# The last block of the down projection: block sizes, order of products, gate, residual and norm weight

## The chip, the cores and the metric

The kernel runs on one NeuronCore of a Trainium2 chip. The metric is device time in microseconds, the median of several executions. The profile is taken from one execution of its own. TensorE multiplies matrices into PSUM, VectorE and ScalarE work element by element on SBUF and PSUM, GpSimd on SBUF; DMAs are issued from SyncE's queue, and accumulating ones from GpSimd's.

## The reference

One layer of a streaming encoder over 512 tokens of width 2048, in float32, and a final RMSNorm. The change touches only its end:

```python
h = modulate(rmsnorm(x, g_norm_ffn[l]), sh2, sc2)
f = (jax.nn.silu(h @ w_ffn_gate[l]) * (h @ w_ffn_up[l])) @ w_ffn_down[l]
x = x + gt2[:, None, :] * f
return rmsnorm(x, g_norm_final)
```

The inner width is 5632. The x of the third line is called x1 here, gt2 is the gate row, and the final norm's weight is g_norm_final.

## The kernel before, in words

**Numbers in two parts.** Every float32 operand is split into hi (rounded to the format that TensorE takes at full rate) and lo (the rest), and a product is three matmuls, hi*hi, hi*lo and lo*hi (`mm3x`, line 938). ScalarE makes hi, VectorE makes lo (`split_into`, line 390); a part of weights is 128x1024.

**Seven products.** Gate, up and down are computed by a 2x2 scheme with seven products for eight (`seven`, line 862). The tokens are two halves (token blocks 0 and 1, and 2 and 3, 128 tokens each), the inner index is taken in groups of 512 (two halves of 256), and two column blocks of 512 make a pass. The left operands are seven tiles per 128 of the inner index. The products are called A11, n1, s2, n4, n3, A12 and A22, in this order; after each, a step named P1, G5, G6, G3, G7, P2 or G4 adds the two PSUM banks that are ready to the sums. The right operands come from four loads and a few sums on VectorE (`b11` to `t4`, lines 889 to 921).

**Down.** Its 11 groups are taken in blocks of `DOWN_BLOCKS` = 3, 3, 3, 2 (line 32). A block loads its left operands from DRAM (14 tiles of 256 KB per group), then makes two passes: columns 0 and 1 (qp = 0), columns 2 and 3 (qp = 1). The sums `fsum[t][q]` (16 tiles of 128x512) stay in SBUF. `later_block` (line 1085) adds each step's banks on VectorE; steps P1, P2 and G4 write column qa of the pass, the others qb. In the last block `finish` (line 1049), after the last addition to a tile, loads x1, multiplies by the gate and adds x1 (both VectorE), and squares with a sum per token (ScalarE). After all blocks the loop at line 1113 makes the norm's factor of each token block (`rstd_from`, line 442, small instructions of VectorE and one square root of ScalarE), multiplies by g_norm_final on GpSimd and by the factor on ScalarE, and stores.

**What sets the order.** Nothing is issued as it is called. `Program` (line 35) records every operation, derives due times backwards from TensorE's order in the program (`deadlines`, line 155), and lays out all five instruction streams with costs of its own (`cost`, line 114, the constants at lines 52 to 62; `schedule`, line 205). An operation goes when its inputs are ready by these costs and its output has a buffer; among those ready at once, the one due first. On the chip each engine then takes its stream in that fixed order. `fits` (line 240) decides whether a tile may be taken ahead of an earlier one of its kind; for hi and lo (3 buffers each) it may not (`IN_ORDER`, line 63, used at line 251). There are 69 buffers of 128x512.

Every instruction of the profile has line 357, where the streams are issued.

## Time and profile before

| | |
|---|---|
| median of 3 runs | 1924.98 us (1924.12 to 1926.82) |
| the profiled execution's own time | 1928.34 us |
| its span, first to last instruction | 1926.5 us |
| TensorE busy | 1813.8 us (94%), mean granted clock 0.978 |
| VectorE busy | 1552.2 us (81%) |
| ScalarE, GpSimd busy | 935.5 us (49%), 216.1 us (11%) |

Down runs from about 1440 to 1897 us of the span. PE is TensorE's matmuls, PEld its weight loads, DVE VectorE, ACT ScalarE, POOL GpSimd, SP SyncE; tiles are named without their numbers, so `b` is any 128x512 tile (sums, gates, x1), `acc` a PSUM bank, `raw` and `araw` loaded weights. The chain of waits follows the end of the program back to what released each step; the timeline lists an engine's instructions by start; instructions overlap by a little, so that the distance of two starts is less than a duration.

### The profile page before, as it was taken

How to read it: one execution, taken by the hardware profiler on the slowest of the kernel's cores; microseconds unless marked ns; L12 is line 12 of the kernel's file. 1: busy time of each engine (PE TensorE's matmuls, PEld its weight loads, DVE VectorE, ACT ScalarE, POOL GpSimd, SP SyncE). 2: the span in 40 equal slices, each digit the busy share in tenths (PEclk: the TensorE clock that was granted, in tenths of full speed). 3: DMA queues.
4: the chain of work that ended last, by engine and by line, in shares of the span. 5: the costliest groups of instructions: out<-in, count | busy, mean ns of one | idle time of the engine just before them, and what ended most of it. 6: DMA issues, size and time to landing. Idle time of an engine off the chain costs nothing.

```text
span 1926.5 us, 22784 instructions
## 1 busy us (share of the span) xinstructions
PE 1813.8 (94%) x8019; PEld 1482.8 (77%) x8019; DVE 1552.2 (81%) x1979; ACT 935.5 (49%) x1213; POOL 216.1 (11%) x192
## 2 busy tenths in 40 slices
PE   3899999899998999999999999999999999999993
PEld 2687877687776788888888788887887888888883
DVE  5897999789869878787877867877667878888898
ACT  6434784432237455454554545545444444333345
POOL 0000045500000010011100111001110000000015
PEclk9999999999998999999999999999999999999997
DMA  9997455599972688678867878876799785675922
GB/s 288 310 336 225 151 187 169 169 316 310 340 233 59 161 211 228 181 225 219 223 179 217 218 184 214 227 189 179 180 302 335 225 283 183 217 263 185 343 88 88
DMA packets 283587, 425.78 MB, mean 221 GB/s; under 512 B 20632, under 2 KB 119632, under 8 KB 283472
## 3 DMA queue, kind: packets, MB, share of 16 engines
q1 hardware_dynamic: 259536, 378.17, 59.4%
q0 software_dynamic: 23936, 46.14, 14.2%
q8 instruction: 63, 1.03, 0.2%
q14 instruction: 52, 0.43, 0.1%
HBM read 374.44 MB, written 49.81 MB: 220 GB/s over the span
## 4 chain that ended last, share of the span: by engine, by line
PE 72%; DVE 14%; DMA 8%; issue 3%; ACT 2%; SPq 1%; POOL 1%; ACTq 0%; DVEq 0%; POOLq 0%
PE acc L357 69%; DVE b L357 10%; DMA araw<-in_w_ada 5%; DVE lo L357 3%; PE mm L357 3%; DMA raw<-in_w_ada 1%; ACT b L357 1%; SPq L357 1%; DMA raw<-in_w_ffn_up 1%; ACT hi L357 1%; DVE araw L357 1%; POOL b L357 1%; DMA f<-b 1%; DMA b<-in_x 0%; DVE s L357 0%
## 5 line engine op out<-in xcount | busy, mean ns | idle before, releaser
L357 PE MATMUL acc<-hi,b 128*128 128x512 f32 x4208 | 1281.9, 393 | 10.3 <-DVE b L357 5.6
L357 PEld LDWEIGHTS acc<-hi,b 128*128 128x128 f32 x4208 | 792.0, 189 | 175.8 <-DVE b L357 7.0
L357 PE MATMUL acc<-lo,b 128*128 128x512 f32 x2104 | 791.8, 393 | 2.0 <-DVE lo L357 1.9
L357 ACT ACTIVATE hi<-raw 128x1024 fp32r<-128x1024 f32 (+2 forms) x289 | 298.7, 1035 | 482.8 <-PE acc L357 382.5
L357 DVE TENSOR_TENSOR lo<-raw,hi 128x1024 fp32r<-128x1024 f32 (+2 forms) x289 | 346.6, 1201 | 148.1 <-ACT hi L357 147.0
L357 PEld LDWEIGHTS acc<-lo,b 128*128 128x128 f32 x2104 | 398.0, 189 | 86.5 <-DVE lo L357 5.0
L357 ACT ACTIVATE hi<-araw 128x1024 fp32r<-128x1024 f32 x264 | 280.1, 1062 | 300.1 <-PE acc L357 270.7
L357 DVE TENSOR_TENSOR lo<-araw,hi 128x1024 fp32r<-128x1024 f32 x198 | 242.3, 1225 | 56.8 <-ACT hi L357 56.1
L357 DVE SCALAR_TENSOR_TENSOR b<-araw,c_act,b 128x512 f32<-128x512 f32 (+1 forms) x315 | 236.4, 756 | 17.1 <-DMA araw<-in_w_ada 12.8
L357 DVE TENSOR_TENSOR b<-b,b 128x512 f32<-128x512 f32 (+4 forms) x318 | 193.1, 635 | 11.7 <-ACT b L357 11.4
L357 PE MATMUL acc<-b,hi 128*128 128x512 f32 x608 | 191.5, 400 | 4.3 <-ACT b L357 3.6
L357 ACT ACTIVATE b<-b 128x512 fp32r<-128x512 f32 (+2 forms) x223 | 128.6, 595 | 83.0 <-DVE b L357 69.2
L357 PEld LDWEIGHTS acc<-b,hi 128*128 128x128 f32 x608 | 115.9, 192 | 30.7 <-ACT b L357 5.7
L357 POOL DMA_DIRECT2D araw<-in_w_ffn_up x44 | 53.1, 1206 | 628.9 <-DVE lo L357 628.1
L357 PE MATMUL acc<-b,lo 128*128 128x512 f32 x304 | 116.2, 396 | 0.7 <-DVE lo L357 0.7
L357 DVE SCALAR_TENSOR_TENSOR lo<-araw,hi 128x1024 fp32r<-128x1024 f32 x66 | 80.6, 1222 | 40.9 <-ACT hi L357 40.7
L357 POOL TENSOR_TENSOR b<-b,b 128x512 f32<-128x512 f32 x32 | 58.0, 1831 | 457.3 <-DVE b L357 430.8
L357 ACT ACTIVATE b<-acc 128x512 f32<-128x512 f32 x142 | 82.3, 593 | 55.0 <-PE acc L357 39.5
L357 DVE TENSOR_TENSOR araw<-araw,raw 128x1024 f32<-128x1024 f32 x88 | 106.9, 1221 | 0.9
L357 POOL DMA_DIRECT2D raw<-in_w_ffn_up x44 | 53.0, 1204 | 315.0 <-DVE lo L357 312.7
L357 DVE SCALAR_TENSOR_TENSOR araw<-araw,raw 128x1024 f32<-128x1024 f32 x66 | 80.0, 1220 | 5.9 <-DMA raw<-in_w_ffn_down 3.2
L357 PE MATMUL mm<-b,hi 128*128 128x512 f32 x192 | 63.3, 410 | 12.4 <-ACT b L357 11.0
(72 smaller groups left out, 909.0 us busy)
## 6 DMA issues: line engine op xcount, KB each, us to landing
araw<-in_w_ada SPq DMA_DIRECT2D x256, 256.0 KB, 5.1
raw<-in_w_ffn_down SPq DMA_DIRECT2D x88, 512.0 KB, 5.2
f<-b SPq DMA_DIRECT2D x154, 256.0 KB, 3.6
b<-f SPq DMA_DIRECT2D x154, 256.0 KB, 6.0
raw<-in_w_ffn_up SPq DMA_DIRECT2D x44, 512.0 KB, 4.5
araw<-in_w_ffn_gate SPq DMA_DIRECT2D x44, 512.0 KB, 3.8
araw<-in_w_ffn_up POOLq DMA_DIRECT2D x44, 512.0 KB, 6.8
raw<-in_w_ffn_gate SPq DMA_DIRECT2D x44, 512.0 KB, 5.1
```

What stands on the lines that cost most here:

```text
L357: getattr(getattr(self.nc, queue), method)(*args, **kw)
```

## The change

The blocks become 2, 3, 3, 3. In the last pass of the last block (`by_tile`) A12 is computed before n3, and A22 first for all groups of token block 2, then of token block 3. For the 12 tiles outside the last pass's column qa, gate, x1, Square and then the multiplication by g_norm_final (VectorE, in place) follow the last addition. For the 4 tiles of that column the sum so far is multiplied by the gate and given x1 ahead of the last product (`residual`), the last product's banks are multiplied by the gate out of PSUM and added, and VectorE scales by factor and norm weight at once. x1 is added by an accumulating DMA from GpSimd's queue. The norm is made for token blocks 0 and 1 together, for 2 and for 3, as each is complete (`norm`); the multiplications on GpSimd go. The rule that hi and lo are taken in order now holds for the tiles of the seven products and no longer for those of `weights` (line 394).

```diff
--- before.py
+++ after.py
@@ -29,7 +29,7 @@
 GROUP_ENDS = (2, 8, 16)
 HELD = 6
 NFF = 5632 // 512
-DOWN_BLOCKS = (3, 3, 3, 2)
+DOWN_BLOCKS = (2, 3, 3, 3)
 BUFS = {"blk": 69, "raw": 6, "araw": 4, "hi": 3, "lo": 3, "acc": 6, "mm": 2}
 SPARE = {"blk": 6}
 
@@ -60,7 +60,6 @@
     RAW_AHEAD = 50.0
     SPARE_AHEAD = 40.0
     SCAN = 8
-    IN_ORDER = ("hi", "lo")
 
     class Queue:
         def __init__(self, prog, name):
@@ -73,7 +72,7 @@
 
     def __init__(self, nc, bufs, spare):
         self.nc, self.bufs, self.spare = nc, bufs, spare
-        self.ops, self.tags = [], {}
+        self.ops, self.tags, self.in_order = [], {}, set()
         for q in self.QUEUES:
             setattr(self, q, self.Queue(self, q))
 
@@ -248,7 +247,7 @@
                 early[tag] = [e for e in early[tag] if e > h]
             if place[name] == h:
                 return True
-            if tag in self.IN_ORDER:
+            if name in self.in_order:
                 return False
             es, at = sorted(early[tag]), 0
             for p in range(h, place[name]):
@@ -859,7 +858,7 @@
         return {"A11": (a11[:, 0:H], a11[:, H:T]), "n1": two(s1h, s1l, 0), "s2": two(s1h, s1l, 1), "n4": two(s2h, s2l, 0),
                 "n3": two(s2h, s2l, 1), "A12": two(fh, fl, 0), "A22": two(fh, fl, 1)}
 
-    def seven(left, b, after, by_dma):
+    def seven(left, b, after, by_dma, by_tile=False):
 
 
         n = len(left) // 2
@@ -869,16 +868,19 @@
             if start:
                 banks[bank] = [mmps("acc") for _ in range(2)]
             for i in range(n):
-                hi, lo = right(i)
-                for k in range(2):
-                    lh, ll = left[2 * i + k][name]
-                    for j in range(2):
-                        cols = slice(j * P, (j + 1) * P)
-                        mm3x(banks[bank][j], (lh[:, cols], ll[:, cols]), (hi[:, k, :], lo[:, k, :]),
-                             start and i + k == 0, stop and i == n - 1 and k == 1)
+                product_of(banks[bank], left[2 * i:2 * i + 2], name, right(i), range(2), start and i == 0, stop and i == n - 1)
+
+        def product_of(bank, pairs, name, right, tiles, start, stop):
+            for k in range(2):
+                lh, ll = pairs[k][name]
+                for j in tiles:
+                    cols = slice(j * P, (j + 1) * P)
+                    mm3x(bank[j], (lh[:, cols], ll[:, cols]), (right[0][:, k, :], right[1][:, k, :]),
+                         start and k == 0, stop and k == 1)
 
         def parts_of(src, sign=1.0):
             hi, lo = stage("hi", 2, 512, F32R), stage("lo", 2, 512, F32R)
+            nc.in_order.update((hi.tensor.name, lo.tensor.name))
             if sign > 0:
                 split_into(src, hi, lo)
             else:
@@ -928,12 +930,23 @@
         after("G6", banks)
         product("n4", "Y", False, True, b22)
         after("G3", banks)
+        if by_tile:
+            product("A12", "Z", True, True, b21)
+            after("P2", banks)
         product("n3", "X", False, True, t3)
         after("G7", banks)
-        product("A12", "Z", True, True, b21)
-        after("P2", banks)
-        product("A22", "X", False, True, t4)
-        after("G4", banks)
+        if not by_tile:
+            product("A12", "Z", True, True, b21)
+            after("P2", banks)
+        if by_tile:
+            parts = [t4(i) for i in range(n)]
+            for j in range(2):
+                for i in range(n):
+                    product_of(banks["X"], left[2 * i:2 * i + 2], "A22", parts[i], (j,), False, i == n - 1)
+                after("G4", banks, (j,))
+        else:
+            product("A22", "X", False, True, t4)
+            after("G4", banks)
 
     def mm3x(ps, l, r, start, stop):
         for i, (x, y) in enumerate(((l[0], r[0]), (l[0], r[1]), (l[1], r[0]))):
@@ -1041,21 +1054,51 @@
             for q in range(4):
                 gfin.append(blk())
                 nc.sync.dma_start(out=gfin[q], in_=a["g_norm_final"][None, q * 512:(q + 1) * 512].broadcast_to([P, 512]))
-            ss = [small(4) for _ in range(NT)]
+            ss = [small(8), small(4), small(4)]
+            ss_of = [ss[0][:, 0:4], ss[0][:, 4:8], ss[1], ss[2]]
 
         for qp in range(2):
             qa, qb = 2 * qp, 2 * qp + 1
 
-            def finish(t, q):
-
+            def gate_of(q):
                 if gt2[q] is None:
                     gt2[q] = blk()
                     nc.sync.dma_start(out=gt2[q], in_=gt2_kept[q])
-                f, o = fsum[t][q], blk()
-                nc.sync.dma_start(out=o, in_=x1_kept[t][q])
-                tt(out=f, in0=f, in1=gt2[q], op=ALU.mult)
-                tt(out=f, in0=f, in1=o, op=ALU.add)
-                nc.scalar.activation(out=o, in_=f, func=AF.Square, accum_out=ss[t][:, q:q + 1])
+                return gt2[q]
+
+            def residual(t, q):
+
+                tt(out=fsum[t][q], in0=fsum[t][q], in1=gate_of(q), op=ALU.mult)
+                nc.gpsimd.dma_start(out=fsum[t][q], in_=x1_kept[t][q], accum_op=ALU.add)
+
+            def finish(t, q, ps=None):
+
+                f = fsum[t][q]
+                if ps is None:
+                    residual(t, q)
+                else:
+                    o = blk()
+                    if t < 2:
+                        tt(out=o, in0=ps, in1=gate_of(q), op=ALU.mult)
+                    else:
+                        stt(out=o, in0=ps, scalar=-1.0, in1=gate_of(q), op0=ALU.mult, op1=ALU.mult)
+                    tt(out=f, in0=f, in1=o, op=ALU.add)
+                nc.scalar.activation(out=blk(), in_=f, func=AF.Square, accum_out=ss_of[t][:, q:q + 1])
+                if not (qp and q == qa):
+                    tt(out=f, in0=f, in1=gfin[q], op=ALU.mult)
+                elif t:
+                    norm(*{1: (0, 1), 2: (2,), 3: (3,)}[t])
+
+            def norm(*tokens):
+                r = rstd_from(ss[max(0, tokens[0] - 1)], len(tokens))
+                for t in tokens:
+                    for i in range(4):
+                        q, f, rt = (qa + i) % 4, fsum[t][(qa + i) % 4], r[:, t - tokens[0]:t - tokens[0] + 1]
+                        if q == qa:
+                            stt(out=f, in0=f, scalar=rt, in1=gfin[q], op0=ALU.mult, op1=ALU.mult)
+                        else:
+                            nc.scalar.activation(out=f, in_=f, func=AF.Copy, scale=rt)
+                        nc.sync.dma_start(out=out[t * P:(t + 1) * P, q * 512:(q + 1) * 512], in_=f)
 
             def add(t, q, ps, op=ALU.add):
                 tt(out=fsum[t][q], in0=fsum[t][q], in1=ps, op=op)
@@ -1082,11 +1125,13 @@
                         fsum[j + 2][qa] = blk()
                         nc.scalar.activation(out=fsum[j + 2][qa], in_=x, func=AF.Copy, scale=-1.0)
 
-            def later_block(step, banks):
-                for j in range(2):
+            def later_block(step, banks, tiles=range(2)):
+                for j in tiles:
                     x, y = banks["X"][j], banks.get("Y", (None, None))[j]
                     if step == "P1":
                         add(j, qa, x, ALU.subtract)
+                        if last and qp:
+                            residual(j, qa)
                     elif step == "G5":
                         add(j + 2, qb, y)
                     elif step == "G6":
@@ -1095,28 +1140,24 @@
                         add(j, qb, y)
                     elif step == "G7":
                         add(j + 2, qb, x)
+                    elif last and qp:
+                        finish(*((j, qa, banks["Z"][j]) if step == "P2" else (j + 2, qa, x)))
                     elif step == "P2":
                         add(j, qa, banks["Z"][j])
                     else:
                         add(j + 2, qa, x, ALU.subtract)
-                    if last and step in ("G3", "G7", "P2", "G4"):
+                    if last and (step in ("G3", "G7") or step in ("P2", "G4") and not qp):
                         finish(*{"G3": (j, qb), "G7": (j + 2, qb), "P2": (j, qa), "G4": (j + 2, qa)}[step])
 
             def b(i, row, column):
                 k = 4 * (n0 + i) + 2 * row
                 return wd[:, k:k + 2, (qa + column) * 512:(qa + column + 1) * 512]
 
-            seven(left, b, later_block if bi else first_block, False)
+            if last and qp:
+                for t in (2, 3):
+                    residual(t, qa)
+            seven(left, b, later_block if bi else first_block, False, by_tile=last and qp == 1)
         n0 += nb
-
-
-    for t in range(NT):
-        r = rstd_from(ss[t])
-        for q in range(4):
-            o = blk()
-            nc.gpsimd.tensor_tensor(out=o, in0=fsum[t][q], in1=gfin[q], op=ALU.mult)
-            nc.scalar.activation(out=o, in_=o, func=AF.Copy, scale=r)
-            nc.sync.dma_start(out=out[t * P:(t + 1) * P, q * 512:(q + 1) * 512], in_=o)
 
     nc.issue()
 
```

## Rows read from the trace of the kernel before

**Rows 1.** The page: its head, part 1 and part 4.

```profile
span 1926.5 us, 22784 instructions
...
PE 1813.8 (94%) x8019; PEld 1482.8 (77%) x8019; DVE 1552.2 (81%) x1979; ACT 935.5 (49%) x1213; POOL 216.1 (11%) x192
...
PE 72%; DVE 14%; DMA 8%; issue 3%; ACT 2%; SPq 1%; POOL 1%; ACTq 0%; DVEq 0%; POOLq 0%
```

**Rows 2.** The chain that ended last, in order of time: start, us, what.

```profile
1779.91 72.55 PE acc L357 x320
...
1896.75 0.08 DVE s L357
```

**Rows 3.** Timeline of PE, the last matmuls: start, us, instruction.

```profile
1895.79 0.61 PE L357 MATMUL acc<-hi,b 128*128 128x512 f32 x2
...
1896.47 0.39 PE L357 MATMUL acc<-hi,b 128*128 128x512 f32 x1
```

**Rows 4.** Stretches: us; busy PE, PEld, DVE, ACT, POOL; PE clock; DMA share; GB/s.

```profile
1460.00:1480.00 20.00, 17.52 (x74) 13.27 (x74) 12.69 (x18) 9.13 (x13) 0.00 (x0) 0.91 0.95 350
...
1580.00:1600.00 20.00, 20.00 (x89) 16.54 (x89) 15.49 (x15) 8.53 (x9) 0.00 (x0) 1.00 1.05 385
...
1780.00:1800.00 20.00, 20.00 (x90) 16.57 (x89) 17.29 (x17) 8.28 (x8) 0.00 (x0) 1.00 0.86 292
...
1840.00:1860.00 20.00, 20.00 (x90) 16.54 (x90) 18.96 (x23) 9.73 (x12) 4.64 (x2) 1.00 0.43 138
1860.00:1880.00 20.00, 20.00 (x89) 16.32 (x88) 20.00 (x23) 7.04 (x9) 2.22 (x1) 1.00 0.15 48
...
sum 477.00, PE 473.62 PEld 389.36 DVE 387.69 ACT 201.91 POOL 18.06; mean PE 19.73 PEld 16.22 DVE 16.15 ACT 8.41 POOL 0.75
```

**Rows 5.** Groups of instructions, 1820.7 to 1896.9: count, busy us, mean ns, idle before.

```profile
L357 DVE TENSOR_TENSOR b<-b,b 128x512 f32<-128x512 f32 x18 | 11.6, 681 | 0.0
```

**Rows 6.** Groups of instructions, 1896.9 to the end.

```profile
L357 DVE TENSOR_TENSOR b<-b,b 128x512 f32<-128x512 f32 x14 | 13.9, 1053 | 0.0
```

**Rows 7.** Timeline of DVE, 1861 to 1918.

```profile
1861.83 2.35 DVE L357 TENSOR_TENSOR araw<-araw,raw 128x1024 f32<-128x1024 f32 x2
...
1893.66 3.09 DVE L357 TENSOR_TENSOR b<-b,b 128x512 f32<-128x512 f32 x5
...
1897.40 1.27 DVE L357 TENSOR_TENSOR b<-b,acc 128x512 f32<-128x512 f32 x2
...
1899.04 7.97 DVE L357 TENSOR_TENSOR b<-b,b 128x512 f32<-128x512 f32 x6
...
1910.29 0.41 DVE L357 SCALAR_TENSOR_TENSOR s<-s,s 128x1 f32<-128x1 f32 x2
...
1916.86 0.16 DVE L357 TENSOR_REDUCE s<-s 128x1 f32<-128x4 f32 x1 [1.94 <-ACT b L357]
...
1917.47 0.16 DVE L357 RECIPROCAL s<-s 128x1 f32<-128x1 f32 x1
```

**Rows 8.** Timeline of POOL, 1895 to 1903.

```profile
1895.62 6.89 POOL L357 TENSOR_TENSOR b<-b,b 128x512 f32<-128x512 f32 x4 [1.92 <-DVE b L357]
```

**Rows 9.** The instructions on tensor out: from a store's issue to its landing.

```profile
DMA to landing us min/median/max: 2.5/2.9/4.0
```

**Rows 10.** DMA issues, 900 to 1400: count, KB each, median us to landing.

```profile
araw<-in_w_ffn_up POOLq DMA_DIRECT2D x28, 512.0 KB, 6.5
```

**Rows 11.** The instructions on tile araw, 1380 to 1400: ns min/median/max, first and last start.

```profile
L357 POOL DMA_DIRECT2D araw<-in_w_ffn_up x4: 1203/1203/1206, 1388.4 to 1397.6; - x4
```

**Rows 12.** Timeline, 1385 to 1402, of DVE.

```profile
1390.69 1.36 DVE L357 TENSOR_TENSOR b<-b,b 128x512 f32<-128x512 f32 x2
```

**Rows 13.** Timeline of ACT, 1907 to the end.

```profile
1907.04 0.63 ACT L357 ACTIVATE b<-b 128x512 f32<-128x512 f32 x1 [0.95 <-DVE b L357]
1907.58 0.19 ACT L357 ACTIVATION_READ_ACCUMULATOR b<-b 128x1 f32 x1
...
1919.84 2.56 ACT L357 ACTIVATE b<-b,s 128x512 f32<-128x512 f32 x4 [1.18 <-DVE s L357]
```

## The prediction

> **What bounds the kernel now.** First the page's head and its chain of waits, to see which engine sets the time. TensorE is busy for 1813.8 of 1926.5 us and holds 72% of the chain; VectorE is busy for 1552.2 and holds 14% [rows 1]. So nearly everywhere the matmuls are the bound, and only where they are not can an edit of VectorE and DMA work pay. The chain in order of time says where that is: from 1779.91 a long piece belongs to TensorE, 72.55 us on it passes to VectorE, and in the last 30 us, from the small norm instructions at 1896.75, no matmul stands in it [rows 2]. TensorE's timeline ends with a matmul that starts at 1896.47 and lasts 0.39, so the matmuls end at **E = 1896.9** and 1926.5 - 1896.9 = **29.6 us of tail** follow. Three matmuls take 0.68 us there (1895.79 to 1896.47), 0.227 each [rows 3], and from 1420 to 1897 TensorE was busy for 473.62 of 477 us [rows 4]: of the time up to E at most those 3.4 us are to be had.
>
> Why is the tail so long? The last block has 2 of the 11 groups: 2 passes x 7 products x 2 groups x 12 matmuls = 336 matmuls, 76.2 us, from 1820.7. In it VectorE was full: 18.96 of 20 us from 1840, 20.00 of 20 from 1860 [rows 4]. Of its 32 instructions for gate and residual 18 ran before E and 14 behind it; those 14 took 13.9 us, 1053 ns each against 681 ns before E [rows 5, 6]. The timelines show why: five of the kind take 3.09 us when GpSimd mostly stands still, and six take 7.97 us from 1899.04, where GpSimd's multiplications by the norm weight run (four from 1895.62 in 6.89 us) [rows 7, 8]. So the tail is a queue of VectorE work, slowed by GpSimd, and behind it one norm, four scalings and the last stores.
>
> **The change, part by part.** *TensorE's work stays.* The sizes 2, 3, 3, 3 add up to the same 11, and the product of the last tokens only has its matmuls in another order. E moves by stalls alone.
>
> *A last block of 3 gives VectorE time.* It now lasts 504 matmuls, 114.2 us. A group in a pass costs VectorE 11 instructions of 1024 columns (7 lo, 4 sums of weights), 1.14 us apart (two take 2.35, each 1.21); the 512-column kind stands 0.60 apart (five in 3.09) [rows 7]. Wide ones: 66 x 1.14 = 75.2 us. Narrow ones of the first pass: 14 additions, 8 gates, 8 norm weights. Of the second, before E: 4 gates of the preceding sums, 6 additions at P1, G5 and G6, 12 at G3 and G7 (addition, gate, weight), 4 at P2, 2 for the first tile of the last product, 2 scalings. Together 60 x 0.60 = 36.0, with some 1.5 us of small norm instructions 112.7 us. That is 99% of 114.2: VectorE stays full, but the queue of 14 does not build up. The price elsewhere: block 1's 42 operand tiles must now arrive within the first block's 76.2 us. That is 10.75 MB beside 4 x 5 x 0.52 = 10.5 MB of weights, 279 GB/s; 385 GB/s was moved at 1580 to 1600 with TensorE busy for 20 of 20 us [rows 4]. I cost it at nothing; if that cover fails, TensorE waits for operands.
>
> *GpSimd's 16 multiplications go.* VectorE does 12 of them before the norm is known, and 4 as part of the scaling. VectorE's narrow work in the block grows by 4 instructions, 2.4 us (counted above), and in return runs at 0.60 instead of about 1.05.
>
> *x1 by DMA.* 16 loads leave SyncE's queue, 16 additions by VectorE go, and GpSimd issues 16 accumulating transfers of 256 KB. No row has such a transfer. Lower bound 2.5 us, the fastest 256 KB store; upper bound 6.5 us, the accumulates of 512 KB in gate and up [rows 9, 10]. I take 4.5: nearest in kind, half the bytes. Each Square, and the norm weight behind it, waits for one; queued behind the Square on ScalarE are the hi copies of the next weights, and for those VectorE's lo and then TensorE. ScalarE is busy for 8.28 of 20 us at 1780 [rows 4], so short waits are covered. On GpSimd nothing else is queued. The planner's own figure is 1.0 + 0.63 + 1.46 + 0.9 = 4.0 us (lines 53, 54 and 120).
>
> The row to weigh here is GpSimd's issue time: 1203 to 1206 ns in all four issues between 1388 and 1398, with two-input VectorE instructions running beside some of them, as from 1390.69 [rows 11, 12]. So I add nothing for VectorE holding them up. [...]
>
> *The order in the last pass.* P2 now comes before n3: from its end two products are left, 2 x 36 x 0.227 = 16.3 us, and tokens 0 and 1 are finished and stored in their shade. The last product runs tile by tile, so token block 2 is complete 18 matmuls = 4.1 us before E. Its three weight parts are then wanted at twice the rate, one per 1.36 us. The third gets its buffer only when n3's last part is done: hi 1.04 (8.28 for 8 at 1780 [rows 4]) + lo 1.21 = 2.25 us against 2.7. That margin of some 0.4 goes as soon as one VectorE instruction stands in front. Bounds 0 and 1.2, one wide instruction; I take a stall of **0.5**, nearer to nothing since the planner orders by due time.
>
> *What is left behind E* is token block 3 alone: gate from PSUM and addition 1.27 (as the two at 1897.40); Square and its read 0.73; mean, square root and reciprocal 0.81 with the gap behind and two small instructions 0.41; three scalings on ScalarE, 3 x 0.64 = 1.92 (the fourth on VectorE beside them); from ScalarE's last end at 1922.40 to the span's end 4.1 [rows 7, 13]. Sum **9.2**. In front of it stands what VectorE owes at E. Between P2's end and E it is asked for: P2 2.4, norm and scaling of two blocks 2.0, G7 3.6, three lo of the last product 3.4, two parts of n3 4.5, first tile and its norm 2.0, in all 17.9 against 16.3: 1.6 late, and block 2's scaling 0.6 behind that. With gaps **2.5**. Bounds: 0 and the 8.2 of the second rival.
>
> **Sum.** New tail 9.2 + 2.5 + 0.5 = 12.2 against 29.6: 17.4 us less. Profiled execution 1928.34 (span 1926.5 and 1.84 around it) to 1910.9. The median shown, 1924.98, lies 3.4 below the profiled one; with the same 17.4 it becomes **1907.6**. Own range of this case: 1903.5 to 1911.
>
> **The rivals.** [...]
>
> *VectorE remains the bound.* At 99% every wait counts. If it loses 5% as in 1840 to 1860 (18.96 of 20 [rows 4]), that is 5.7 us of 114.2, and the queue at E is 2.5 + 5.7 = 8.2: 1913.3, up to 1916.5 where stalls of the last product come on top. For it: each norm weight now waits on a Square that waits on a transfer. Against: the next 20 us were full to 20.00.
>
> *The plan changes elsewhere.* The rule that hi and lo are taken in order now holds for the seven products only, so the program need not keep its early order. TensorE stood 112.7 us in all, 29.6 of it in the tail and 3.4 after 1420, so some 80 us of early waits could grow or shrink. Against: weights there arrive in the order in which they are wanted, so I see no reason to reorder. If a sixth of those 80 were added, 13 us: 1921, about no change.
>
> *Slower: the accumulates come late.* The instruction streams are fixed by the planner, which counts 4.0 us. Parts are made about one part, 12 matmuls or 2.7 us, ahead; so from a landing of 4.0 + 2.7 = 6.7 us on, ScalarE, standing at a Square, holds hi back from TensorE. Twelve of the transfers lie before the last product. At an excess of 2.5 us each TensorE loses 30 us: 1907.6 + 30 = 1937.6. For it: 6.5 is measured at 512 KB, and the wait is new. Against: these have half the bytes, and the DMA share at 1860 to 1880 was 0.15.
>
> **How the numbers follow.** Forecast 0.66, better still 0.08, VectorE remains the bound 0.14, plan changes 0.06, slower by accumulates 0.06. A measurement of this kernel can tell about 0.2%, 3.9 us, from no change. The first three and half of the fourth are faster: 0.91. Within 0.2%: the other half of the fourth and a little of the last, 0.04. Slower: 0.05. The range, 1903 to 1916.5, holds the forecast's and the second rival's and some of the first's, over 8 in 10.
>
> **What would show it.** Right: the last matmul within 1 us of 1896.9; behind it VectorE has a handful of narrow instructions near 0.68 us, no GpSimd multiplication; 12 stores issued before or just after it; 10 to 15 us from there to the end. The step of the accumulates is right if they land in 4 to 5 us and no hi waits on a Square. Wrong: waits of TensorE for lo or hi in the last 114 us, ten or more narrow VectorE instructions behind E, or a different timeline before 1436.

## The result, and the profile after

The changed kernel takes **1908.27 us** (median of 6 runs, 1899.48 to 1917.1) against 1924.04 for the kernel before on the same chip (6 runs, 1921.53 to 1926.82). The ratio is **0.9911 [0.989, 0.9933]**: faster, by 15.8 us where 17.4 were forecast. The total came out 0.7 us from the forecast. The steps behind it did not: two large errors cancel, and that the total was met is luck.

The profiled execution took 1899.48 us. Every instruction has line 356 now. The page's head, part 1 and part 4 answer to [rows 1]:

```profile
span 1897.7 us, 22755 instructions
...
PE 1805.7 (95%) x8019; PEld 1471.6 (78%) x8019; DVE 1544.1 (81%) x1978; ACT 930.7 (49%) x1208; POOL 197.8 (10%) x192
...
PE 73%; DVE 13%; DMA 8%; ACT 3%; issue 3%; SPq 0%; POOL 0%; ACTq 0%; DVEq 0%
```

The last matmuls on PE's timeline, as [rows 3]:

```profile
1884.81 0.62 PE L356 MATMUL acc<-hi,b 128*128 128x512 f32 x2
...
1885.49 0.39 PE L356 MATMUL acc<-hi,b 128*128 128x512 f32 x1
```

So E is 1885.88, and 11.8 us of tail follow where 29.6 stood before. Three matmuls take 0.68 us here too, 0.227 each for 512 columns; with a mean granted clock of 1.00 from 1880 to 1886, that is what "full rate" stands for where hi is introduced. To see what happened ahead of E, a mark is needed that both kernels share. I take **M**, the start of the last accumulating load of gate and up on GpSimd's queue. Up to there the change edits nothing. The two rows, from POOL's timeline of the kernel before and then of the changed one:

```profile
1430.78 1.20 POOL L357 DMA_DIRECT2D raw<-in_w_ffn_up  x1 [1.51 <-DVE lo L357]
```

```profile
1411.78 1.19 POOL L356 DMA_DIRECT2D raw<-in_w_ffn_up  x1 [1.52 <-DVE lo L356]
```

**Three distances tell the story.** M came 19.0 us earlier, in a part of the program that the change does not touch. A part of that may be the choice of execution: the profile of the change is the fastest of its six runs, and that of before (1928.34) is slower than all of its six. The stretch from 60 us to M, in the columns of [rows 4], before and then changed:

```profile
60.00:1430.80 1370.80, 1326.34 (x5877) 1084.21 (x5876) 1113.35 (x1470) 683.40 (x886) 180.87 (x152) 0.98 0.76 217
```

```profile
60.00:1411.80 1351.80, 1313.18 (x5876) 1072.18 (x5875) 1111.27 (x1469) 681.93 (x885) 179.86 (x152) 0.99 0.76 220
```

The matmuls are the same but for one. They took 13.2 us less at a higher mean granted clock (0.99 for 0.98), and TensorE stood still for 5.8 us less.

From M to E took 474.1 us instead of 466.1, so TensorE lost 8.0 there. The tail lost 17.8. The forecast had 0, +0.5 and -17.9 (its 17.4 has the stall of 0.5 in it).

The tail is as predicted. These are VectorE's full-width instructions behind E, beside [rows 6, 7]; the eight scalings of ScalarE are the other part, and GpSimd has no multiplication left:

```profile
1885.74 0.69 DVE L356 TENSOR_TENSOR b<-b,b 128x512 f32<-128x512 f32 x1 [0.60 <-ACT b L356]
...
1886.43 0.68 DVE L356 SCALAR_TENSOR_TENSOR b<-acc,b 128x512 f32<-128x512 f32 x1
...
1887.14 0.69 DVE L356 TENSOR_TENSOR b<-b,b 128x512 f32<-128x512 f32 x1
...
1888.45 0.75 DVE L356 SCALAR_TENSOR_TENSOR b<-b,s,b 128x512 f32<-128x512 f32 x1
...
1890.59 0.75 DVE L356 SCALAR_TENSOR_TENSOR b<-b,s,b 128x512 f32<-128x512 f32 x1
```

That is a handful near 0.68 us, where 14 of 1053 ns stood. ScalarE's last scalings end at 1892.53, 5.2 us before the span's end:

```profile
1889.81 2.72 ACT L356 ACTIVATE b<-b,s 128x512 f32<-128x512 f32 x4
```

The 8.0 us between M and E are waits of TensorE's weight loads. PEld's timeline from 1480 on, with all its waits over 0.15 us:

```profile
1481.06 0.19 PEld L356 LDWEIGHTS acc<-hi,b 128*128 128x128 f32 x1 [0.40 <-ACT b L356]
...
1484.73 0.30 PEld L356 LDWEIGHTS acc<-lo,b 128*128 128x128 f32 x2 [0.84 <-DVE lo L356]
...
1628.91 0.19 PEld L356 LDWEIGHTS acc<-lo,b 128*128 128x128 f32 x1 [0.33 <-DVE lo L356]
...
1721.88 0.30 PEld L356 LDWEIGHTS acc<-lo,b 128*128 128x128 f32 x2 [0.39 <-DVE lo L356]
...
1825.15 0.19 PEld L356 LDWEIGHTS acc<-lo,b 128*128 128x128 f32 x1 [0.22 <-DVE lo L356]
...
1840.37 0.19 PEld L356 LDWEIGHTS acc<-hi,b 128*128 128x128 f32 x1 [1.97 <-ACT hi L356]
...
1841.63 0.19 PEld L356 LDWEIGHTS acc<-lo,b 128*128 128x128 f32 x1 [1.07 <-DVE lo L356]
...
1876.66 0.30 PEld L356 LDWEIGHTS acc<-hi,b 128*128 128x128 f32 x2 [1.80 <-ACT hi L356]
...
1879.01 0.19 PEld L356 LDWEIGHTS acc<-lo,b 128*128 128x128 f32 x1 [0.20 <-DVE lo L356]
```

They sum to 7.2 us. The kernel before has a single one in the same stretch, of 0.34. The first four (2.0 us) stand inside the passes of the three blocks before the last one, the other five (5.3 us) in the last block. Behind the wait at 1840 the mean granted clock falls too:

```profile
1840.00:1860.00 20.00, 18.87 (x75) 15.20 (x76) 19.52 (x22) 8.46 (x11) 4.29 (x5) 0.91 0.46 84
1860.00:1880.00 20.00, 18.59 (x82) 14.98 (x81) 19.64 (x30) 11.06 (x17) 2.55 (x3) 1.00 0.44 89
```

These two stretches [rows 4] had TensorE at 20.00 of 20 before, at clock 1.00. After the two stands of 1.97 and 1.07 us the mean granted clock was 0.68 from 1842 to 1844 and 0.50 from 1844 to 1846; from 1848 it was 1.00 again.

### The profile page after: what moved, and what is told of

Same layout as the page of the kernel before. It is cut to its first block, busy times and chain, and to the rows that moved or that the text cites. A ratio compares the mean times of both kernels' runs of the same rounds, so it can differ in the third digit from the quotient of the medians.

```text
span 1897.7 us, 22755 instructions
## 1 busy us (share of the span) xinstructions
PE 1805.7 (95%) x8019; PEld 1471.6 (78%) x8019; DVE 1544.1 (81%) x1978; ACT 930.7 (49%) x1208; POOL 197.8 (10%) x192
## 4 chain that ended last, share of the span: by engine, by line
PE 73%; DVE 13%; DMA 8%; ACT 3%; issue 3%; SPq 0%; POOL 0%; ACTq 0%; DVEq 0%
PE acc L356 70%; DVE b L356 9%; DMA araw<-in_w_ada 4%; PE mm L356 3%; DVE lo L356 3%; ACT b L356 2%; DMA raw<-in_w_ffn_down 1%; ACT hi L356 1%; DMA raw<-in_w_ffn_up 1%; DMA f<-b 1%; DMA raw<-in_w_ada 1%; DVE araw L356 0%; SPq L356 0%; DMA b<-f 0%; DMA raw<-in_w_in 0%
## 5 line engine op out<-in xcount | busy, mean ns | idle before, releaser
L356 PE MATMUL acc<-hi,b 128*128 128x512 f32 x4208 | 1270.0, 392 | 12.7 <-DVE b L356 6.0
L356 PE MATMUL acc<-lo,b 128*128 128x512 f32 x2104 | 780.7, 392 | 2.3 <-DVE lo L356 2.3
L356 ACT ACTIVATE hi<-raw 128x1024 fp32r<-128x1024 f32 (+2 forms) x289 | 298.6, 1034 | 472.5 <-PE acc L356 405.1
L356 DVE SCALAR_TENSOR_TENSOR b<-araw,c_act,b 128x512 f32<-128x512 f32 (+1 forms) x315 | 236.1, 755 | 15.7 <-DMA araw<-in_w_ada 11.3
L356 DVE TENSOR_TENSOR b<-b,b 128x512 f32<-128x512 f32 (+4 forms) x318 | 188.5, 617 | 14.6 <-ACT b L356 14.0
L356 DVE TENSOR_TENSOR b<-acc,b 128x512 f32<-128x512 f32 x94 | 61.5, 684 | 15.9 <-PE acc L356 15.7
```

What stands on the lines that cost most here:

```text
L356: getattr(getattr(self.nc, queue), method)(*args, **kw)
```

## The experiments

Every run has its M and E in the profile. This table is worked out from those rows. "Waits" is the sum of TensorE's weight-load waits over 0.15 us from 65 us after M on, as listed above. The offset is where the 69 buffers of 128x512 and the weight buffers behind them start in each partition, as the built program lays them out.

| run | median us | ratio to before | offset in bytes | M | M to E | waits | tail |
|---|---|---|---|---|---|---|---|
| before | 1922.98 to 1924.66 | | 21184 | 1430.8 | 466.1 | 0.3 | 29.6 |
| the change | 1908.27 | 0.9911 [0.989, 0.9933] | 20992 | 1411.8 | 474.1 | 7.2 | 11.8 |
| again | 1905.86 | 0.9906 [0.9885, 0.9928] | 20992 | 1413.8 | 476.5 | 10.4 | 11.3 |
| sizes_only | 1937.11 | 1.0068 [1.0047, 1.0089] | 21184 | 1428.9 | 468.5 | 3.2 | 37.4 |
| old_sizes | 1907.26 | 0.9916 [0.9886, 0.9945] | 20992 | 1424.5 | 470.6 | 4.2 | 19.4 |
| old_order | 1906.38 | 0.9911 [0.9888, 0.9933] | 20992 | 1419.4 | 471.1 | 5.4 | 15.7 |
| before_shifted | 1911.90 | 0.9939 [0.9919, 0.996] | 21504 | 1422.1 | 466.0 | 0.7 | 29.5 |
| after_shifted | 1916.08 | 0.9951 [0.9933, 0.9969] | 21184 | 1427.9 | 472.5 | 8.7 | 11.8 |
| x1_by_vector | 1916.71 | 0.9958 [0.9942, 0.9973] | 20992 | 1420.6 | 468.2 | 2.5 | 26.8 |
| late_plan | 1901.86 | 0.9888 [0.9862, 0.9915] | 20992 | 1413.4 | 472.4 | 7.8 | 12.8 |
| swap_off | 1907.21 | 0.9916 [0.9895, 0.9936] | 20992 | 1414.3 | 473.6 | 8.4 | 14.0 |
| combined | 1903.96 | 0.9896 [0.9875, 0.9917] | 20992 | 1416.8 | 470.9 | 4.9 | 14.3 |
| x1_by_dma_alone | 1925.50 | 1.0006 [0.9992, 1.0021] | 21184 | 1428.9 | 476.5 | 8.1 | 21.9 |
| weight_by_vector_alone | 1917.27 | 0.9967 [0.9956, 0.9979] | 21184 | 1423.6 | 466.9 | 0.7 | 24.6 |

### Is the time before M the execution's or the kernel's? (again)

The changed kernel once more, with no edit.

> The changed kernel once more, unedited: what belongs to the change and what to the execution. In the first two profiles the last accumulating load of gate and up is issued at 1430.8 (before) and at 1411.8 us (changed), 19 us apart, though the instruction streams are the same up to there; from it to the end it is 495.7 us before and 485.9 us changed. My theory: the change is worth what happens behind that point, 9 to 15 us, and the time up to it belongs to the execution, so this profile has a tail of 11 to 13 us behind the last matmul again, 483 to 490 us from that point to the end, and the median is 10 to 16 us below before. Rival: the early part is shorter in the changed kernel itself; then that point comes near 1412 us again and the median is more than 20 us below before.

M came at 1413.8 again, so two profiles of this kernel agree, and the theory that the early arrival belongs to one execution falls. The median, some 17 us below before, lies between theory and rival. Yet the engines' streams are the same in both kernels up to M (but for the order of a few x1 stores on SyncE's queue). What differs is the program's layout: six small constants fewer, 32 bytes each in every partition, and all large buffers start 192 bytes lower.

### The layout by itself (before_shifted, after_shifted)

An unused tile moves the buffers of the kernel before onto a multiple of 512 bytes, and those of the changed kernel to where the kernel before had them. No instruction changes its place.

```diff
# before_shifted: kernel before
     tiny = small(1)
+    pad = const.tile([P, 80], F32, name="pad")
# after_shifted: changed kernel
     tiny = small(1)
+    pad = const.tile([P, 48], F32, name="pad")
```

> The kernel before with one unused constant tile of 320 bytes per partition ahead of the large buffers and nothing else: the same instruction streams, but the 85 large SBUF buffers start at a multiple of 512 bytes, as they do in the changed kernel, and no longer 192 bytes behind one (the change dropped six small tiles of 32 bytes each, which moved every buffer behind them). Theory now: this shift is a part of the measured gain. DMA then moves 348 to 356 GB/s at 96 to 144 us, as in the changed kernel, for 336; the last accumulating load of gate and up is issued at 1412 to 1424 us for 1430.8; the tail of 29.6 us stays; the median is 6 to 10 us below before. Rival: the earlier arrival belongs to something else in the changed kernel or to chance; then the rate stays at 334 to 336 GB/s and the median within 2.5 us of before.

> The changed kernel with one unused constant tile of 192 bytes per partition, so that the large buffers lie 192 bytes behind a multiple of 512 again, as before the change; the instruction streams are those of the changed kernel. Theory now: it loses what the shift gave, 6 to 10 us, and stands at 1912 to 1917 us, 7 to 11 below before, with a tail of 11 to 13 us and 486 to 491 us from the last accumulating load of gate and up to the end. Rival: it stays within 2.5 us of the changed kernel, at 1904 to 1911 us.

The kernel before gains 0.6% by the tile alone, 11 to 12 us; the changed one loses some 8 to 10 without its shift (1916.08 against 1905.86 and 1908.27). The stretch from 96 to 144 us shows what becomes of the transfers. Its columns are those of [rows 4]; first the kernel before, then before_shifted, then the changed one, then after_shifted:

```profile
96.00:144.00 48.00, 47.88 (x212) 39.39 (x211) 44.80 (x83) 16.21 (x24) 0.00 (x0) 1.00 1.09 336
```

```profile
96.00:144.00 48.00, 47.87 (x215) 39.39 (x214) 46.72 (x85) 15.33 (x23) 0.00 (x0) 1.00 1.04 348
```

```profile
96.00:144.00 48.00, 47.88 (x213) 39.26 (x212) 45.77 (x84) 16.38 (x25) 0.00 (x0) 1.00 1.04 350
```

```profile
96.00:144.00 48.00, 48.00 (x202) 39.31 (x203) 43.80 (x84) 14.44 (x21) 0.00 (x0) 0.94 1.05 327
```

Divide the last column by the one before it: 308 and 311 GB/s per unit of DMA time with the offset of 21184, 335 and 337 on the multiple of 512. The same bytes take about 8% less DMA time, in a stretch that is full of transfers. All 14 profiles fall into these two groups: 306 to 311 with the offset, 331 to 339 on the multiple. In this stretch itself no wait of TensorE is saved by it (busy for 47.9 to 48.0 of 48 us in each); from 60 us to M TensorE stood still for 44.5 us before and 40.2 in before_shifted, 38.6 in the change and 44.8 in after_shifted. How the faster transfers lead to that is not shown. The nine profiles on the multiple have M between 1411.8 and 1424.5 (middle 1416.8), the five others between 1423.6 and 1430.8 (middle 1428.9).

So the edit itself, with the layout held, is worth 0.9951 [0.9933, 0.9969], **7 to 9 us** (7 by the medians, 9 by the ratio), and not 16. From M to the end the profiles say about the same, 8 to 11 us: 495.7 us before, 485.9, 487.8 and 484.4 in the change, again and after_shifted.

### The block sizes (sizes_only, old_sizes)

The kernel before with the new sizes, and the changed kernel with the old ones.

```diff
# sizes_only: kernel before
-DOWN_BLOCKS = (3, 3, 3, 2)
+DOWN_BLOCKS = (2, 3, 3, 3)
# old_sizes: changed kernel
-DOWN_BLOCKS = (2, 3, 3, 3)
+DOWN_BLOCKS = (3, 3, 3, 2)
```

> The kernel before with block sizes 2, 3, 3, 3 and nothing else. My theory: the third group in the last block gives VectorE the time that it lacked; asked for 75.2 us of wide and 36 us of narrow work in 114.2 us it has no queue at the last matmul but the last product's own 6 narrow instructions (3.6 us instead of 9.6 and more); behind it remain norms, 8 scalings of 0.64 us and 4.1 us of store: a tail of 15 to 18 us instead of 29.6, and no stall of TensorE for late accumulates, so 10 to 14 us faster than before. Rival: order, gate ahead of the last product and GpSimd's release carry the gain, and sizes alone give less than 5 us (tail over 24 us).

> The changed kernel with the old block sizes 3, 3, 3, 2. My theory: VectorE is asked for 50.2 us of wide and some 37.5 us of narrow and small work in 76.2 us, so some 11 us of it stand behind the last matmul or hold TensorE up: tail 18 to 23 us, or up to 8 us of more waits of TensorE in the last 80 us; slower than the changed kernel by 7 to 12 us. Rival: the order of the last pass and the accumulates make the gain; then it is within 4 us of the changed kernel.

sizes_only fell the wrong way: 13 us slower. The larger last block was to give VectorE time for gate and x1 ahead of E. Instead those tiles come late. With 42 operand tiles and 16 sums, 58 of the 69 buffers are taken, and gates, norm weights and x1 are loaded only when the last pass gives buffers back. SyncE's queue shows it:

```profile
1869.57 1.37 SPq L357 DMA_DIRECT2D b<-gt  x3
1870.98 0.42 SPq L357 DMA_DIRECT2D b<-x  x1
1871.45 0.48 SPq L357 DMA_DIRECT2D b<-in_g_norm_final  x1
...
1875.78 8.49 SPq L357 DMA_DIRECT2D b<-x  x13
```

In the kernel before, norm weights are issued from 1815 and x1 from 1800. No run has more buffers, so that this reason is argued, from the count and the queue. So VectorE has 13 more of the narrow kind behind E (1897.48), beside 12 multiplications of GpSimd. From DVE's and then POOL's timeline of sizes_only:

```profile
1898.12 7.51 DVE L357 TENSOR_TENSOR b<-b,b 128x512 f32<-128x512 f32 x7
...
1905.99 9.68 DVE L357 TENSOR_TENSOR b<-b,b 128x512 f32<-128x512 f32 x6
```

```profile
1900.15 19.09 POOL L357 TENSOR_TENSOR b<-b,b 128x512 f32<-128x512 f32 x12 [470.01 <-DVE b L357]
```

That is 1.1 to 1.6 us each, and a tail of 37.4. In the changed kernel the old sizes give a tail of 19.4 and fewer waits. From M to the end that is 490.0 against 485.9 and 487.8, and in the medians nothing that can be told apart. The sizes also have a price that I had put at nothing: sizes_only has 3.2 us of TensorE waits, inside the passes of its first three blocks, where the kernel before has 0.3. Ahead of two of the five, VectorE had waited for a load of weights, 2.26 us at 1643.74 and 2.62 at 1758.99. Behind the second TensorE waits 0.88 us, at 1761.41. VectorE's row:

```profile
1758.99 1.23 DVE L357 SCALAR_TENSOR_TENSOR araw<-araw,raw 128x1024 f32<-128x1024 f32 x1 [2.62 <-DMA raw<-in_w_ffn_down]
```

SyncE's queue had issued 15 operand tiles between 1730.58 and 1751.2, ahead of those weights and among them; that these held the weights up is likely and not shown.

### x1 loaded and added by VectorE (x1_by_vector)

The changed kernel with x1 as before.

```diff
-                nc.gpsimd.dma_start(out=fsum[t][q], in_=x1_kept[t][q], accum_op=ALU.add)
+                o = blk()
+                nc.sync.dma_start(out=o, in_=x1_kept[t][q])
+                tt(out=fsum[t][q], in0=fsum[t][q], in1=o, op=ALU.add)
```

> The changed kernel with x1 loaded by SyncE's queue and added by VectorE, instead of accumulated by DMA from GpSimd's queue. Theory: the 16 additions are 9.6 us more for a VectorE that is busy for 97% of the last block; they stand in front of the parts of weights or behind the last matmul: 4 to 9 us slower than the changed kernel, though the wait of TensorE for a Square that waits for x1 (3.0 us at 1840 in the changed kernel) is gone. Rival: the late accumulates were the dearest item; then it is 2 to 4 us faster than the changed kernel.

It is 9 us slower, about the 16 additions, but the profile gives the same reason as in sizes_only. The loads wait for buffers, VectorE does 14 narrow instructions in one piece at 1883.78, and more than that behind E (1888.76). SyncE's queue, then VectorE's timeline:

```profile
1864.61 1.85 SPq L356 DMA_DIRECT2D b<-in_g_norm_final  x4
1866.51 10.07 SPq L356 DMA_DIRECT2D b<-x  x13
```

```profile
1883.78 8.51 DVE L356 TENSOR_TENSOR b<-b,b 128x512 f32<-128x512 f32 x14
```

What the accumulating transfer buys in this kernel is a buffer: it lands in the sum and needs no tile of its own. Without it the changed kernel has a tail of 26.8 us in place of 11.8. That a buffer is what counts is argued from the queue, as above.

### One part in the kernel before (x1_by_dma_alone, weight_by_vector_alone)

```diff
# x1_by_dma_alone, in finish of the kernel before
-                f, o = fsum[t][q], blk()
-                nc.sync.dma_start(out=o, in_=x1_kept[t][q])
+                f = fsum[t][q]
                 tt(out=f, in0=f, in1=gt2[q], op=ALU.mult)
-                tt(out=f, in0=f, in1=o, op=ALU.add)
-                nc.scalar.activation(out=o, in_=f, func=AF.Square, accum_out=ss[t][:, q:q + 1])
+                nc.gpsimd.dma_start(out=f, in_=x1_kept[t][q], accum_op=ALU.add)
+                nc.scalar.activation(out=blk(), in_=f, func=AF.Square, accum_out=ss[t][:, q:q + 1])
# weight_by_vector_alone: behind that Square, and in the final loop
+                tt(out=f, in0=f, in1=gfin[q], op=ALU.mult)
...
-            o = blk()
-            nc.gpsimd.tensor_tensor(out=o, in0=fsum[t][q], in1=gfin[q], op=ALU.mult)
+            o = fsum[t][q]
```

> The kernel before with x1 accumulated by DMA from GpSimd's queue and nothing else (sizes 3, 3, 3, 2, buffers 192 bytes behind a multiple of 512 as before). Theory: x1_by_vector says that the accumulates are the dearest part; here they take 16 additions (9.6 us) off VectorE, so that of the 14 narrow instructions behind the last matmul at most 4 stay: tail 17 to 21 us for 29.6, 1910 to 1915 us. Rival: the Squares now wait for the transfers, and GpSimd's multiplications, behind the transfers' issue, still slow VectorE: tail 24 us or more, less than 6 us faster than before.

> The kernel before with the norm weight multiplied in by VectorE behind each Square, in place, and no work on GpSimd at the end; nothing else. Theory: VectorE is full, so its 16 more narrow instructions all land behind the last matmul, but run at 0.60 us apart instead of 1.05: about 28 of them, 17 us, then one norm, scalings and stores: tail 25 to 29 us, 0 to 5 us faster than before. [...]

The first gains nothing (1.0006): the tail falls by 7.7 us and E comes 10.4 later. Ten of GpSimd's 16 multiplications now start ahead of E (five before), and VectorE's wide instructions beside them take twice their time. VectorE's timeline of x1_by_dma_alone, one row of GpSimd's, then the wait of TensorE that follows:

```profile
1869.79 2.58 DVE L357 TENSOR_TENSOR lo<-araw,hi 128x1024 fp32r<-128x1024 f32 x1
1872.29 2.31 DVE L357 TENSOR_TENSOR araw<-araw,raw 128x1024 f32<-128x1024 f32 x1
...
1879.08 1.21 DVE L357 TENSOR_TENSOR lo<-raw,hi 128x1024 fp32r<-128x1024 f32 x1
```

```profile
1872.06 3.69 POOL L357 TENSOR_TENSOR b<-b,b 128x512 f32<-128x512 f32 x2 [0.79 <-PE acc L357]
```

```profile
1879.21 0.19 PEld L357 LDWEIGHTS acc<-lo,b 128*128 128x128 f32 x1 [3.20 <-DVE lo L357]
```

The second is the one part that pays alone, 0.9967: VectorE takes 16 instructions more, and still the tail falls by 5.0 us, since without GpSimd its narrow ones stand 0.60 apart, as seven from 1899.76 in 4.30 us:

```profile
1899.76 4.30 DVE L357 TENSOR_TENSOR b<-b,b 128x512 f32<-128x512 f32 x7
```

### The order of the last pass (old_order, swap_off)

old_order gives the last pass its old order of products and tiles; swap_off puts only A12 back behind n3 and keeps the tile order.

```diff
# old_order: changed kernel
-            seven(left, b, later_block if bi else first_block, False, by_tile=last and qp == 1)
+            seven(left, b, later_block if bi else first_block, False, by_tile=False)
# swap_off: changed kernel
-        if by_tile:
-            product("A12", "Z", True, True, b21)
-            after("P2", banks)
         product("n3", "X", False, True, t3)
         after("G7", banks)
-        if not by_tile:
-            product("A12", "Z", True, True, b21)
-            after("P2", banks)
+        product("A12", "Z", True, True, b21)
+        after("P2", banks)
```

> The changed kernel with the last pass in the old order (n3, then A12, then A22 for both token blocks together). My theory: the last product then ends for token blocks 2 and 3 at once, so two gates, additions, Squares and norms stand behind the last matmul: a tail 3 to 5 us longer (15 to 17 us); TensorE in return does not wait 1.8 us for the parts of the last product that the order by token block wants at double rate. In sum 1 to 4 us slower than the changed kernel. Rival: the order is what shortens the tail; then the tail is over 20 us and the kernel 8 us or more slower than the changed one.

> The changed kernel with A12 back behind n3 in the last pass; the last product still goes by token block. In the changed kernel TensorE waits 1.8 to 2.3 us at the start of the last product. Theory: n3 and A22 add into the same bank X, and with A12 gone from between them A22 has to wait until VectorE has read n3's result out of the bank (step G7; at 1875.87 to 1876.55 in the changed kernel, the first matmul at 1876.66). With A12 between them that wait is gone (under 0.5 us), and so is the one for late weights ahead of n3 (0.2 to 1.4 us); token blocks 0 and 1 end 8.2 us later, so the tail grows by 0 to 2 us. In sum 0 to 4 us faster than the changed kernel, 481 to 487 us from the last accumulating load of gate and up to the end. Rival: the wait comes from the parts of the last product that are wanted at double rate; then 1.5 us or more of it stays at the start of the last product.

old_order's tail is 15.7, some 4 us longer, and its M to E 3 to 5 shorter: no gain in the end, 1906.38. swap_off was aimed at the wait at 1876.66. A22 adds into the bank that n3 has just left, and with A12 moved ahead of n3 nothing stands between the two any more. Before A22 may write there, VectorE's G7 addition has to read the bank. VectorE's timeline of the changed kernel:

```profile
1871.66 3.09 DVE L356 TENSOR_TENSOR b<-b,b 128x512 f32<-128x512 f32 x5
1874.67 1.22 DVE L356 TENSOR_TENSOR lo<-araw,hi 128x1024 fp32r<-128x1024 f32 x1
...
1875.87 0.68 DVE L356 TENSOR_TENSOR b<-b,acc 128x512 f32<-128x512 f32 x1
```

The addition ends at 1876.55 and the weight load starts at 1876.66. The row names hi as the releaser, but the hi of A22's first part (ScalarE, start 1873.29, 1.05 long; its lo is the row at 1874.67) was done at 1874.34. In swap_off that wait is gone. In its place lo is late at the start of the last product and twice within it, for 0.77, 0.65 and 1.37, and the waits sum to 8.4:

```profile
1877.40 0.30 PEld L356 LDWEIGHTS acc<-lo,b 128*128 128x128 f32 x2 [0.77 <-DVE lo L356]
...
1883.27 0.19 PEld L356 LDWEIGHTS acc<-lo,b 128*128 128x128 f32 x1 [1.37 <-DVE lo L356]
```

So the rival, late parts of the last product, is not gone either: with the bank out of the way it costs 2.8 us. VectorE is full, and what is taken off one place comes up at another.

### The accumulates' lateness (late_plan, combined)

late_plan tells the planner that these 16 transfers land 3 us later than it thought. combined adds swap_off and loads ScalarE's table for the square root early (the load takes 1.28 us, at 1875.91 in the changed kernel).

```diff
# late_plan: changed kernel
+    X1_LATE = 3.0
...
+        op["late"] = op["dma"] and op["q"] == "POOL" and len(outs[0].shape) == 2
...
-                end = dma_free + self.DMA_LAND
+                end = dma_free + self.DMA_LAND + (self.X1_LATE if op["late"] else 0.0)
# combined: both edits, and in the last block
+            nc.scalar.activation(out=sqrt_ready, in_=tiny, func=AF.Sqrt, after=gfin[0])
```

> The changed kernel with one figure of the planner: it counts 3 us more until an accumulated x1 has landed (7.0 us for 4.0; measured 4.0 to 8.2, median 4.7). The streams differ behind gate and up only. Theory: the Squares are laid out later, ScalarE no longer stands 6.9 us at one, TensorE's waits of 2.0 + 1.1 us at 1840 go, and the time from the last accumulating load of gate and up to the end falls from 486 to 488 to 481 to 485 us: 2 to 5 us faster than the changed kernel. Rival: the wait only moves, since VectorE has no time left in the last block: within 2 us of the changed kernel.

> swap_off, with the planner counting 3 us more for an accumulated x1 (as in late_plan) and the table of the square root loaded at the start of the last block. Theory: the waits of TensorE in the last 114 us, 6 to 7 us in the changed kernel, fall under 2 us, the tail stays at 12 to 14 us, 478 to 483 us from the last accumulating load of gate and up to the end: 4 to 8 us faster than the changed kernel, 1897 to 1902 us. Rival: VectorE is full in the last block, so what is taken off one wait comes back at another; then it is within 2.5 us of late_plan and 483 to 487 us.

What it is about, in the changed kernel: the instructions on tile x, from issue to landing and who waited, then ScalarE's timeline at 1838.

```profile
L356 POOL DMA_DIRECT2D b<-x x16: 841/854/1132, 1803.3 to 1880.6; - x16
...
  ACT b L356: 24.4, 10
...
DMA to landing us min/median/max: 4.0/4.7/8.2
```

```profile
1838.65 0.63 ACT L356 ACTIVATE b<-b 128x512 f32<-128x512 f32 x1 [6.86 <-DMA b<-x]
...
1839.28 2.94 ACT L356 ACTIVATE hi<-araw 128x1024 fp32r<-128x1024 f32 x3
```

ScalarE stood at a Square for 6.86 us, three hi copies were queued behind it, and TensorE waited 1.97 and 1.07. late_plan takes that wait away. Another comes: a weight load is late, VectorE waits 1.36 for it, and TensorE 2.41 (PEld's timeline of late_plan):

```profile
1869.90 0.19 PEld L358 LDWEIGHTS acc<-lo,b 128*128 128x128 f32 x1 [2.41 <-DVE lo L358]
...
1876.51 0.30 PEld L358 LDWEIGHTS acc<-hi,b 128*128 128x128 f32 x2 [1.75 <-ACT hi L358]
```

From M to the end it takes 485.2 us, the change 485.9 and 487.8. Its median, 1901.86, is the lowest measured, but its interval overlaps that of the change. combined has the shortest waits of the kernels with the new sizes and the accumulates (4.9 in all) and gives them back in the tail, 14.3. No version was found that can be told from the changed kernel.

## Why the prediction was right and wrong

**The bound and the tail: right.** VectorE's queue behind E, slowed by GpSimd, was the tail, and it went: 12.2 forecast, 11.8 and 11.3 measured. VectorE was nearly full up to E, as reckoned (19.52 and 19.64 of 20 us from 1840 on; 111.0 us in the last block for 112.7). That the sum came so near is partly luck. The queue in front of token block 3 was 0.5 us, with another 0.5 for block 2's scaling ahead of the small instructions, in place of 2.5; from ScalarE's end to the span's end it took 5.2 in place of 4.1; and the 0.5 of stall stands ahead of E and not in the tail.

**"E moves by stalls alone ... I take a stall of 0.5": this step failed.** E relative to M moved by 8.0, and by 10.4 and 6.4 in again and after_shifted. Three terms were mis-sized:

- *The block sizes, "I cost it at nothing".* sizes_only, which has nothing else, shows 3.2 us of waits and E 2.4 later from M; in the change four such waits make 2.0. I had looked at the transfers as a rate over a whole block, and let the cover hold. Single loads of weights came late all the same (VectorE waited 2.26 and 2.62 us for two), and elsewhere lo and a copy of an operand did.
- *The accumulates, "I take 4.5".* The middle was right (4.7), the spread was not thought of: up to 8.2. The rival "the accumulates come late" had its decision point at 6.7 us; it was passed, and the mechanism ran as described, at 3.0 us in place of 30.
- *The last product.* I had looked for the stall in t4's weight parts. It was the PSUM bank: moving A12 away puts A22 right behind n3 on the same bank, 1.80 us in the change, 2.28 in again. The parts are late too once the bank is free: 2.8 us in swap_off, for bounds of 0 to 1.2.

Common to the last two: with VectorE busy for 39.2 of the 40 us from 1840 there is no slack, and the second rival ("VectorE remains the bound") has 5.7 where the last block lost 5.3. But the loss stands ahead of E, as TensorE's waits, and not as a queue behind it. Two signs of being wrong that were on record came true: waits of TensorE for lo and hi in the last 114 us, and a last matmul that is not within 1 us of 1896.9 (it ends 11 us earlier, by the early part).

**The early part: not seen.** I had a rival for a changed plan before 1436, through the rule of hi and lo. That plan is the same, and yet M moved. I had read what the change does to instructions and not what it does to the layout. In medians the layout is worth 0.9939 [0.9919, 0.996].

So the sum reads: -17.8 of tail, +6 to +10 of waits, -8 to -12 of layout, for -17.9, +0.5 and 0 on record. That is -15 to -23, and the medians gave -15.8. The total held because the last two nearly cancel, which nothing in the prediction foresaw.

**The chance of 0.08 for "better still".** No run shows the time that it stands for. In the first 65 us from M on TensorE was busy for 61.85 us in the change, with 28 operand tiles in its first block, and for 61.76 us before, with 42, at a mean granted clock of 0.97 in both.

**GpSimd's issue, right as far as it was measured.** No delay by VectorE shows in the issue: 854 ns in the middle, 1132 at most, with VectorE full beside them. The landings spread from 4.0 to 8.2 us, and no run says why, so that a delay between issue and start is not excluded.

**Each part's share.** The norm weight on VectorE pays alone (0.9967). x1 by DMA does not (1.0006), nor the sizes (1.0068). Inside the change x1 by DMA does pay (0.9911 with it, 0.9958 without), where GpSimd multiplies no longer beside VectorE. The sizes are worth nothing that can be told even there (old_sizes 0.9916), nor is the order in the last pass (0.9911).

**Open.** The runs of the changed kernel spread over 17.6 us (1899.48 to 1917.1), those of before over 5.3. The mean granted clock goes with it: 0.990 in the shortest run of the changed kernel, 0.984 in the longest, and shorter runs tend to have the higher clock in every kernel but sizes_only. Which of the two comes first no run says. M differs by 12.7 us among kernels with the same offset, so the layout is not all that moves it. The norm weight on VectorE with the buffers on the multiple of 512 was not tried; by the product of the two ratios, 0.9967 x 0.9939 = 0.9906, an estimate, those two edits alone would equal the whole change.

## What to carry to other kernels

When a stage's tail is cut, look at what the work that was moved ahead now delays: on an engine that is already full it can come back as somebody's wait (here VectorE was busy for 39.2 of the 40 us from 1840, and TensorE waited for 5.3 us in the last block). Before a measured gain is put down to an edit, pick a mark that the edit can't reach and compare the times up to it; if they differ, compare the memory layout and shift it by itself. Test each part alone and also without each part, since a part that is worth nothing alone (x1 by DMA here) can be worth something beside another.

## What was not expected of the hardware

**The start of the buffers.** An offset of 192 bytes past a multiple of 512 cost 8 to 9% more DMA time per byte in a stretch full of loads, 41 of 53 of 256 KB (336 GB/s at share 1.09 against 348 at 1.04), and 0.6% of the whole kernel. The runs have only this one offset, so they don't show which boundary counts. Nearly all packets of the stretch are under 2 KB (17744 of 18515 before). By what mechanism the offset costs DMA time no run shows.

**VectorE beside GpSimd.** 128x1024 instructions with two inputs took 2.31 and 2.58 us with GpSimd multiplying beside them and 1.21 without, in x1_by_dma_alone. At 128x512 the mean was 1053 ns behind E, where GpSimd multiplies, against 681 ns ahead of it, where GpSimd mostly stands still, in the kernel before. Why they slow down no run shows.
